# A new start for a Strassen ReGLU kernel: x rows and three weight columns plain on one queue, three plain blocks, second x half in quarter steps

## Chip, cores, metric

One core of one Trainium2 chip. The metric is the device time of one execution in microseconds (us), median of several runs. The engines are named as the profile names them: PE (TensorE), DVE (VectorE), ACT (ScalarE), POOL (GpSimd), SP (the queue of the sync engine). PEld is weight loading.

## The reference

```python
# x: 16 x 256 x 512, w1: 512 x 4096, w2: 2048 x 512, all float32
h = x @ w1
gate, value = np.split(h, 2, axis=-1)
h = np.maximum(gate, 0) * value
return (h @ w2).astype(np.float32)
```

## The kernel before

The 4096 rows of x are done in four sets of 1024. Everything is cast to f16. Both products are done by a Strassen form with seven products instead of eight: sums of weight quarters (T1 to T4) and of x quarters (S1 to S4) are formed first, and a "Block" for one column of 128 gates and 128 values then takes 14 matmuls of 512 columns. A "Plain" block needs no sums and takes 16. The first set begins with plain blocks, because the sums take time. What a block yields, max(gate, 0) times value, is called g; the second product needs sums of g in the same way, here "g sums". In the lines of the profile, wr are the plain weights and wt their sums, x_A the plain quarters of x and x_S their sums, g_S the sums of g (at the start these buffers, and g, also hold loaded float32 data); W, X and Y are the accumulators that PE writes.

```python
WX = {"P1": ("B11", "A11"), "P2": ("B21", "A12"), "P3": ("B22", "S4"), "P4": ("T4", "A22"),
      "P5": ("T1", "S1"), "P6": ("T2", "S2"), "P7": ("T3", "S3")}       # weight, x
SLOT = {"P1": 0, "P5": 1, "P2": 3, "P6": 4, "P3": 5, "P7": 9, "P4": 13}  # a block every 7 slots
SUMS = (("S1", "A21", "A22", SUB), ("S2", "S1", "A11", SUB), ("S4", "A12", "S2", ADD), ("S3", "A11", "A21", SUB))
# ... cut ...
NFILL = 2
NPLAIN = 4
CHUNKS = ((0, 2), (2, 2), (4, 2), (6, 2), (8, 4), (12, 4))     # weight columns by chunk
```

The x sums of the first set are made by VectorE, each a sum of two SBUF tensors of 128 x 1024 f16. The start of the first set, shortened:

```python
for i in range(2):                                   # SP queue, float32
    nc.sync.dma_start(out=xf[:, 2 * i:2 * i + 2], in_=x_v[0, :, 2 * i:2 * i + 2])
    nc.sync.dma_start(out=wl[:, :, i], in_=w1_v[:, :, i, :2 * P])
nc.gpsimd.tensor_copy(out=gate, in_=xf[:, 0, :1])    # GpSimd's casting loads wait for the first x
fetch_w1(1, 0); fetch_w1(1, 1)                       # casting loads on GpSimd's queue
# ... second half of x, casting, then the other chunks of w1 ...
# ... casts, transposes, plain blocks of the first x half ...
for p in plain:                                      # second x half, four plain blocks
    # ... matmuls ...
    x_sum(xo)                                        # VectorE: one of S1, S2, S4, S3
    if p is not plain[-1]:
        p.close(1)
    look_x(0, p.jb)
```

GpSimd makes the weight sums of the first set, and issues the loads of w2 between them:

```python
w1_ops(nc.gpsimd, 4, 2)       # T1..T4 for columns 4 and 5: four instructions of 128 x 512
fetch_w2(0)
fetch_w2(1)
w1_ops(nc.gpsimd, 6, 2)
fetch_w2(2)
fetch_w2(3)
w1_ops(nc.gpsimd, 8, 2)
w1_ops(nc.gpsimd, 10, 2)
# ... copies of w2 ...
for t in TURNS:
    w1_one(nc.gpsimd, 12, 4, *t)
    if t[0] == "T2":
        add_w2("T1", "B12"); add_w2("T3", "B22")
add_w2("T2", "T1")
cast_x(1)
# ... later, at P2 of columns 11, 13, 15 (h = 0, 2, 4): sums for the second matmul
for m in ("S1", "S3")[:2 - h // 4]:
    g_sum(nc.gpsimd, go, m, h, h + 2)
# ... and at the end of the set:
g_sum(nc.vector, go, "S1", 6, 8)
for m in ("S2", "S4"):
    for h in (0, NHC // 2):
        g_sum(nc.vector, go, m, h, h + NHC // 2)
g_sum(nc.vector, go, "S3", NHC // 2, NHC)
```

Of the kernel before, what the change touches and what calls it, by code (L numbers as in the profile page):

```python
# [20 lines left out]
NFILL = 2  # L21
NPLAIN = 4
# [77 lines left out]
def fast_way(ctx, tc, x2, w1, w2, out2, flag):  # L100
# [26 lines left out]
    CHUNKS = ((0, 2), (2, 2), (4, 2), (6, 2), (8, 4), (12, 4))  # L127
# [27 lines left out]
    def w1_ops(eng, jb, n):  # L155
        for t in TURNS:
            w1_one(eng, jb, n, *t)
# [37 lines left out]
    class Block:  # L195
        def __init__(self, xo, g, jb):
            self.xo, self.g, self.jb = xo, g, jb
# [46 lines left out]
    class Plain:  # L244
        def __init__(self, g, jb):
            self.g, self.jb = g, jb

        def open_x(self):
            self.X = psx.tile([P, TH], F32, name="X", tag="X")

        def open_w(self):
            self.W = psw.tile([P, TH], F32, name="W", tag="W")

        def mm(self, side, a, q, n=1):
            ts = slice(q * 256, (q + n) * 256)
            ps = self.W if side else self.X
            for e in range(4):
                name = (("B11", "B21"), ("B12", "B22"))[side][e // 2]
                nc.tensor.matmul(ps[:, ts], W(name, self.jb)[:, e % 2], a[:, e, ts], start=e == 0, stop=e == 3,  # L259
                                 skip_group_check=True)  # L260

        def close(self, h):
            v = tmp.tile([P, 2, TH], F32, name="v", tag="tmp")[:, 0]
            nc.scalar.activation(v, self.W, COPY, scale=GS)
            nc.vector.scalar_tensor_tensor(out=self.g[:, self.jb, h * TH:(h + 1) * TH], in0=self.X, scalar=0.0,
                                           in1=v, op0=MAX, op1=MULT)
# [12 lines left out]
    def mm2_stream(s, go):  # L279
# [14 lines left out]
        def step(name, b):  # L294
# [19 lines left out]
            elif name == "P3":  # L314
# [3 lines left out]
                nc.sync.dma_start(out=out_v[s, 0, b], in_=d["o1"])  # L318
# [48 lines left out]
    xf = go["S1"].rearrange("p a t -> p (a t)").bitcast(F32).rearrange("p (b d) -> p b d", b=NB)  # L367
    xh = go["S2"][:, :NB]
    wl = g[:, NJ - 4:].rearrange("p a t -> p (a t)").bitcast(F32).rearrange("p (e g j) -> p e g j", e=4, g=2)

    def turn_pair(o, b0):
        for b in (b0, b0 + 1):
            ps = psw.tile([P, 4, P], F32, name="W", tag="W")
            for e in range(4):
                nc.tensor.transpose(ps[:, e], xf[:, b, e * P:(e + 1) * P], ident[F32])
            copy = nc.scalar.copy if b % 2 else nc.vector.tensor_copy
            copy(out=o["A1"][:, :, b * P:(b + 1) * P], in_=ps)  # L377

    def turn_half(o, b0, copy):
        ps = psx.tile([P, 4, 2, P], F16, name="X", tag="X")  # L380
# [9 lines left out]
    def cast_w(g_):  # L390
        nc.scalar.copy(out=wr[0][:, :2, g_], in_=wl[:, :2, g_])
        nc.vector.tensor_copy(out=wr[0][:, 2:, g_], in_=wl[:, 2:, g_])  # L392
# [12 lines left out]
    for i in range(2):  # L405
        nc.sync.dma_start(out=xf[:, 2 * i:2 * i + 2], in_=x_v[0, :, 2 * i:2 * i + 2])  # L406
        nc.sync.dma_start(out=wl[:, :, i], in_=w1_v[:, :, i, :2 * P])
    for t in ident.values():
        make_identity(nc, t)
    nc.gpsimd.tensor_copy(out=gate, in_=xf[:, 0, :1])  # L410
    fetch_w1(1, 0)
    fetch_w1(1, 1)
    for b in (0, 2):
        nc.gpsimd.dma_start(out=xh[:, b:b + 2], in_=x_v[0, :, NB + b:NB + b + 2])
# [5 lines left out]
    plain = [Plain(g, jb) for jb in range(NPLAIN)]  # L420
    idle(NWARM)
    cast_w(0)
    turn_pair(xo, 0)
    idle(NFILL)
    plain[0].open_x()
    plain[1].open_x()
    for p in plain[:2]:
        p.mm(0, xo["A1"], 0)
    cast_w(1)
    turn_pair(xo, 2)  # L430
    for p in plain[:2]:
        p.open_w()
        p.mm(1, xo["A1"], 0)
    for p in plain[:2]:
        p.mm(0, xo["A1"], 1)
        p.mm(1, xo["A1"], 1)
        p.close(0)
    for p in plain[2:]:
        p.open_x()
        p.open_w()  # L440
        p.mm(0, xo["A1"], 0, 2)
        p.mm(1, xo["A1"], 0, 2)
        p.close(0)
        if p is plain[2]:
            turn_half(xo, 0, nc.vector.tensor_copy)
    turn_half(xo, 2, nc.scalar.copy)
# [6 lines left out]
    for p in plain:  # L453
        p.open_x()
        p.open_w()
        if p is plain[0]:
            for q in range(2):
                p.mm(0, xo["A2"], q)
                p.mm(1, xo["A2"], q)
        else:  # L460
            p.mm(0, xo["A2"], 0, 2)
            p.mm(1, xo["A2"], 0, 2)
        x_sum(xo)
        if p is not plain[-1]:
            p.close(1)
        look_x(0, p.jb)

    def look_w1(i):
        c, o = place[i // 2 * 2]
        look(wr[c][:, :, i % 2, o * P:(o + 2) * P], NX + i, 1024)  # L470
# [27 lines left out]
    LOOKS[0, NPLAIN].insert(0, lambda: plain[-1].close(1))  # L498
# [15 lines left out]
    for s in range(NS):  # L514
# [4 lines left out]
        plan = {jb * PERIOD + at: (jb, n) for jb in blocks for n, at in SLOT.items()}  # L519
        last = NJ * PERIOD  # L520
        stream = mm2_stream(s, go)
        if s == 0:
            w1_ops(nc.gpsimd, 4, 2)
            fetch_w2(0)
            fetch_w2(1)
            w1_ops(nc.gpsimd, 6, 2)
# [53 lines left out]
        if s + 1 < NS:  # L580
# [9 lines left out]
            if s == 0:  # L590
                w1_ops(nc.vector, 0, 2)
                w1_ops(nc.vector, 2, 2)
# [33 lines left out]
```

## Time and profile before

| | before |
|---|---|
| median of three runs | 312.16 us (311.8 to 312.37) |
| span of the profiled run | 310.2 us |
| PE busy | 301.7 us |
| granted PE clock | 1.0 |

From the profile's page of the kernel before, the busy time of each engine and the chain that ended last by engine:

```profile
PE 301.7 (97%) x1867; PEld 183.0 (59%) x1867; DVE 216.4 (70%) x330; ACT 189.0 (61%) x450; POOL 148.3 (48%) x135
...
PE 92%; DMA 2%; DVE 2%; issue 1%; ACT 1%; SPq 0%; DVEq 0%
```

PE is busy 97% of the span, and the chain that ended last is 92% PE. What can be won lies in PE's few waits. The timeline of PE shows them; its columns are start in us, length in us, engine, line, operation, output and inputs, count, and in brackets the idle time before it with what ended it. Kernel before, PE's timeline:

```profile
10.68 1.03 PE L259 MATMUL W<-x_A,wr 128*128 128x256 f16 x8 [1.51 <-DVE x_A L377]
...
18.95 0.60 PE L259 MATMUL X<-x_A,wr 128*128 128x256 f16 x4 [0.27 <-ACT x_A L384]
...
25.43 0.59 PE L202 MATMUL W<-x_S,wt 128*128 128x512 f16 x2
26.25 0.59 PE L202 MATMUL X<-x_A,wr 128*128 128x512 f16 x2 [0.23 <-ACT Y L209]
...
27.54 0.59 PE L202 MATMUL X<-x_A,wr 128*128 128x512 f16 x2
```

The stalls are 1.51, 0.27 and 0.23 us. Matmuls of 512 start every 0.216 us, so a product of two takes 0.432. P5 of column 4 (25.43) is its second product, P2 (26.25) its third, and P1 of column 5 starts at 27.54.

Kernel before, VectorE's timeline, its four x sums S1, S2, S4, S3 (written x_S):

```profile
18.93 1.54 DVE L451 TENSOR_TENSOR x_S<-x_A 128x1024 f16<-128x1024 f16 x1 [0.21 <-ACT x_A L384]
...
21.25 0.78 DVE L451 TENSOR_TENSOR x_S<-x_S,x_A 128x1024 f16<-128x1024 f16 x1
...
22.98 0.68 DVE L451 TENSOR_TENSOR x_S<-x_A,x_S 128x1024 f16<-128x1024 f16 x1
...
24.71 0.68 DVE L451 TENSOR_TENSOR x_S<-x_A,x_A 128x1024 f16<-128x1024 f16 x1
```

GpSimd's timeline over the same stretch, weight sums (wt) and the issue of two w2 loads:

```profile
19.88 1.60 POOL L160 TENSOR_TENSOR wt<-wr 128x512 f16<-128x512 f16 x1
21.44 1.60 POOL L160 TENSOR_TENSOR wt<-wr,wt 128x512 f16<-128x512 f16 x1
22.99 1.81 POOL L356 DMA_DIRECT2D w<-in_w_dram  x2
24.80 1.59 POOL L160 TENSOR_TENSOR wt<-wr 128x512 f16<-128x512 f16 x1
26.47 1.15 POOL L160 TENSOR_TENSOR wt<-wr,wt 128x512 f16<-128x512 f16 x1
```

S1 took 1.54 us. GpSimd's sums of the same shape took 1.15 to 1.16 us when undisturbed, and 1.60, 1.60 and 1.59 where a VectorE sum had begun before them.

### The profile page before, as it was taken

To read this page: it belongs to the slowest core of one execution; us is meant where nothing else is said; L and a number is where in the kernel's file an instruction comes from. 1 tells how busy PE (TensorE), PEld (TensorE's weight loads), DVE (VectorE), ACT (ScalarE), POOL (GpSimd) and SP (SyncE) were. 2 spreads that over 40 slices of the span, in tenths; PEclk is the share of its full clock that TensorE was granted. 3 is DMA by queue.
4 is the path that set the end of the run, shared out by engine and by line. 5 is a ranking of instruction groups with operands and counts; after the bars stand their busy time and mean duration, and the time that the engine had idled before them with its cause. 6 is when DMAs were issued, how large, how long until landed. Compare 5 with 4: busy or idle time off the path is not lost.

```text
span 310.2 us, 5097 instructions
## 1 busy us (share of the span) xinstructions
PE 301.7 (97%) x1867; PEld 183.0 (59%) x1867; DVE 216.4 (70%) x330; ACT 189.0 (61%) x450; POOL 148.3 (48%) x135
## 2 busy tenths in 40 slices
PE   8899999999999999999999999999999999999993
PEld 4654444588854444478874444458884444448883
DVE  1376888898548888884338888886526888888311
ACT  3347767647677667648847667656857667673230
POOL 5779997950003537992001435995000433898000
PEclk9999999999999999999999999999999999999999
DMA  7999979998315370045220110028311100000113
GB/s 246 200 202 204 215 195 231 203 120 231 121 73 101 71 169 0 3 92 158 90 104 35 34 34 2 0 52 151 139 71 68 34 6 30 0 2 0 69 68 139
DMA packets 33449, 30.74 MB, mean 99 GB/s; under 512 B 13872, under 2 KB 27952, under 8 KB 33200
## 3 DMA queue, kind: packets, MB, share of 16 engines
q0 software_dynamic: 10704, 11.54, 23.1%
q1 hardware_dynamic: 22576, 18.75, 20.5%
q8 instruction: 15, 0.25, 0.4%
q10 hardware_dynamic: 144, 0.13, 0.1%
q14 instruction: 10, 0.08, 0.1%
HBM read 24.12 MB, written 11.53 MB: 115 GB/s over the span
## 4 chain that ended last, share of the span: by engine, by line
PE 92%; DMA 2%; DVE 2%; issue 1%; ACT 1%; SPq 0%; DVEq 0%
PE Y L202 25%; PE X L202 17%; PE W L202 17%; PE Y L286 13%; PE W L286 8%; PE X L286 8%; DMA g<-in_w_dram 2%; PE W L259 2%; PE X L259 2%; DVE g_S L275 1%; ACT x_A L384 0%; SPq L406 0%; DVE wr L392 0%; DVE g L241 0%; DVE x_A L377 0%
## 5 line engine op out<-in xcount | busy, mean ns | idle before, releaser
L275 POOL TENSOR_TENSOR g_S<-g 128x512 f16<-128x512 f16 (+1 forms) x47 | 60.5, 1330 | 125.3 <-DVE g L241 123.4
L202 PEld LDWEIGHTS <-wt 128*128 128x128 f16 x480 | 46.9, 98 | 55.0 <-issue 0.2
L202 PE MATMUL X<-x_A,wr 128*128 128x512 f16 x240 | 71.4, 379 | 0.2 <-ACT Y L209 0.2
L202 PE MATMUL Y<-x_S,wt 128*128 128x512 f16 x240 | 71.4, 379 | 0.0
L202 PEld LDWEIGHTS <-wr 128*128 128x128 f16 x360 | 35.2, 98 | 41.1 <-issue 0.5
L229 DVE SCALAR_TENSOR_TENSOR cc<-W,pu 128x512 f32<-128x512 f32 x60 | 41.5, 692 | 23.8 <-ACT pu L223 23.7
L209 ACT COPY Y<-X 128x512 f32<-128x512 f32 x60 | 34.2, 570 | 37.7 <-PE X L202 37.1
L286 PEld LDWEIGHTS <-g_S 128*128 128x128 f16 x512 | 49.9, 98 | 6.4 <-DVE g_S L275 0.6
L235 DVE SCALAR_TENSOR_TENSOR cc<-Y,pu 128x512 f32<-128x512 f32 x60 | 41.5, 691 | 6.2 <-PE Y L202 0.2
L223 ACT ACTIVATE pu<-Y 128x512 f32<-128x512 f32 x60 | 35.8, 597 | 14.3 <-PE Y L202 14.3
L230 DVE SCALAR_TENSOR_TENSOR g<-X,cc 128x512 f16<-128x512 f32 x60 | 41.5, 691 | 2.3
L286 PEld LDWEIGHTS <-g 128*128 128x128 f16 x384 | 37.6, 98 | 8.2
L241 DVE SCALAR_TENSOR_TENSOR g<-Y,cc 128x512 f16<-128x512 f32 x60 | 40.8, 681 | 1.8 <-PE Y L202 1.8
L216 ACT ACTIVATE pu<-W 128x512 f32<-128x512 f32 x60 | 36.1, 602 | 0.0
L202 PE MATMUL W<-x_S,wr 128*128 128x512 f16 x120 | 35.7, 379 | 0.0
L202 PE MATMUL W<-x_S,wt 128*128 128x512 f16 x120 | 35.7, 379 | 0.0
L202 PE MATMUL Y<-x_A,wt 128*128 128x512 f16 x120 | 35.7, 379 | 0.0
L286 PE MATMUL X<-w,g 128*128 128x256 f16 x256 | 31.2, 272 | 0.0
L286 PE MATMUL Y<-v,g_S 128*128 128x256 f16 x256 | 30.6, 273 | 0.0
L316 DVE SCALAR_TENSOR_TENSOR o<-W,pv 128x256 f32<-128x256 f32 x16 | 6.8, 423 | 30.4 <-PE W L286 30.4
L275 POOL TENSOR_TENSOR g_S<-g,g_S 128x512 f16<-128x512 f16 x18 | 21.8, 1210 | 1.4
L275 POOL TENSOR_TENSOR g_S<-g_S,g 128x512 f16<-128x512 f16 x18 | 21.3, 1186 | 1.4
(69 smaller groups left out, 297.4 us busy)
## 6 DMA issues: line engine op xcount, KB each, us to landing
out_dram<-o SPq DMA_DIRECT2D x16, 256.0 KB, 2.2
out_dram<-pv SPq DMA_DIRECT2D x15, 256.0 KB, 2.0
x<-in_x_dram POOLq DMA_DIRECT2D x3, 1024.0 KB, 8.0
xn<-x SPq DMA_DIRECT2D x12, 256.0 KB, 3.2
wr<-in_w_dram POOLq DMA_DIRECT2D x4, 512.0 KB, 14.5
w<-in_w_dram POOLq DMA_DIRECT2D x4, 512.0 KB, 11.8
wr<-in_w_dram POOLq DMA_DIRECT2D x6, 256.0 KB, 8.8
g_S<-in_x_dram SPq DMA_DIRECT2D x2, 512.0 KB, 4.7
```

The lines of the kernel that those rows point to most:

```text
L202: nc.tensor.matmul(ps, W(wn, self.jb)[:, b], self.xo[xn][:, b, :], start=fresh and b == 0, stop=b == 1, skip_group_check=True)
L209: nc.scalar.copy(out=self.Y, in_=self.X)
L216: nc.scalar.activation(self.p5, self.W, COPY, scale=GS)
L223: nc.scalar.activation(self.u2, self.Y, COPY, scale=-GS)
L229: nc.vector.scalar_tensor_tensor(out=self.c12, in0=self.W, scalar=GS, in1=self.u2, op0=MULT, op1=ADD)
L230: nc.vector.scalar_tensor_tensor(out=self.g[:, self.jb, :TH], in0=self.X, scalar=0.0, in1=self.c12, op0=MAX, op1=MULT)
L235: nc.vector.scalar_tensor_tensor(out=self.c22, in0=self.Y, scalar=-GS, in1=self.p5, op0=MULT, op1=ADD)
L241: nc.vector.scalar_tensor_tensor(out=self.g[:, self.jb, TH:], in0=self.Y, scalar=0.0, in1=self.c22, op0=MAX, op1=MULT)
L259: nc.tensor.matmul(ps[:, ts], W(name, self.jb)[:, e % 2], a[:, e, ts], start=e == 0, stop=e == 3, skip_group_check=True)
L275: eng.tensor_tensor(go[n][:, h0:h1], go[i0][:, h0:h1], go[i1][:, h0:h1], op=op)
L286: nc.tensor.matmul(ps, go[gn][:, k, b * P:(b + 1) * P], V[vn][:, k, :], start=fresh and k == 0, stop=k == NHC - 1, skip_group_check=True)
L316: nc.vector.scalar_tensor_tensor(out=d["o1"][:, HALF:], in0=d["W"], scalar=1 / GS, in1=d["pu"][:, 1], op0=MULT, op1=ADD)
```

## The change

The intent: have the matmuls start without waiting for a load in the wrong order, and use one plain block fewer. All x rows of the first set and three weight columns come as float32 on the SP queue in order of use, and are cast on chip; three blocks are plain instead of four; the second half of x is used in quarter steps as it arrives; P1 of the first Strassen block (column 3) is done before the last plain values. The core of the diff, cut:

```diff
-NFILL = 2
-NPLAIN = 4
+NFILL = 1
+NPLAIN = 3
-    CHUNKS = ((0, 2), (2, 2), (4, 2), (6, 2), (8, 4), (12, 4))
+    CHUNKS = ((0, 2), (2, 1), (3, 2), (5, 3), (8, 4), (12, 4))
+    for b in (0, 2):
+        nc.sync.dma_start(out=xf[:, b:b + 2], in_=x_v[0, :, b:b + 2])
+    fetch_wl(0, 0)
+    fetch_wl(1, 0)
+    fetch_wl(0, 1, 2)
+    nc.sync.dma_start(out=xg[:, :2], in_=x_v[0, :, NB:NB + 2])
+    fetch_wl(2, 0)
+    fetch_wl(2, 1)
+    nc.sync.dma_start(out=xg[:, 2:], in_=x_v[0, :, NB + 2:])
-    nc.gpsimd.tensor_copy(out=gate, in_=xf[:, 0, :1])
+    nc.gpsimd.tensor_copy(out=gate, in_=wl[0][:, 0, 1, :1])
 # ... cut: the start ...
+    whole[0].values()
+    whole[0].close()
+    cast_w(2, 0)
+    whole[1].values()
+    nc.vector.tensor_copy(out=xh[:, :2], in_=xg[:, :2])
+    turn_half(xo, 0, nc.vector.tensor_copy)
+    whole[1].close()
+    cast_w(2, 1)
+    nc.scalar.copy(out=xh[:, 2:], in_=xg[:, 2:])
+    part(whole[2])
+    part(parts[0][0])
+    part(parts[0][1])
+    turn_half(xo, 2, nc.scalar.copy)
+    part(parts[0][2])
+    x_sum(xo)
+    for p in parts[1][:2]:
+        part(p)
+        x_sum(xo)
+        look_x(0, p.jb)
+    parts[1][2].gates()
+    lead.P1()
+    parts[1][2].values()
+    look_x(0, 2)
+    x_sum(xo)
 # ... cut: GpSimd's order ...
-            w1_ops(nc.gpsimd, 4, 2)
+            w1_ops(nc.gpsimd, 3, 2)
             fetch_w2(0)
             fetch_w2(1)
-            w1_ops(nc.gpsimd, 6, 2)
+            w1_ops(nc.gpsimd, 5, 3)
 # ... cut: the stores of the last set are split in two ...
```

More of the change, by code (lines that the diff above doesn't have):

```diff
@@ L244, in fast_way, with __init__, mm, gates @@
     class Plain:
-        def __init__(self, g, jb):
-            self.g, self.jb = g, jb
-        def open_x(self):
-            self.X = psx.tile([P, TH], F32, name="X", tag="X")
-        def open_w(self):
-            self.W = psw.tile([P, TH], F32, name="W", tag="W")
-        def mm(self, side, a, q, n=1):
-            ts = slice(q * 256, (q + n) * 256)
-            ps = self.W if side else self.X
-            for e in range(4):
-                name = (("B11", "B21"), ("B12", "B22"))[side][e // 2]
-                nc.tensor.matmul(ps[:, ts], W(name, self.jb)[:, e % 2], a[:, e, ts], start=e == 0, stop=e == 3,
-                                 skip_group_check=True)
-        def close(self, h):
-            v = tmp.tile([P, 2, TH], F32, name="v", tag="tmp")[:, 0]
-            nc.scalar.activation(v, self.W, COPY, scale=GS)
-            nc.vector.scalar_tensor_tensor(out=self.g[:, self.jb, h * TH:(h + 1) * TH], in0=self.X, scalar=0.0,
-                                           in1=v, op0=MAX, op1=MULT)
+        def __init__(self, g, jb, a, h, q, n):
+            self.g, self.jb, self.a, self.at, self.q = g, jb, a, h * TH, range(q, q + n)
+            self.t = slice(q * HALF, (q + n) * HALF)
+        def mm(self, ps, names, q):
+            ts = slice(q[0] * HALF, q[-1] * HALF + HALF)
+            for e in range(4):
+                nc.tensor.matmul(ps[:, ts], W(names[e // 2], self.jb)[:, e % 2], self.a[:, e, ts], start=e == 0,
+                                 stop=e == 3, skip_group_check=True)
+        def gates(self, q=None):
+            if q is None or q[0] == self.q[0]:
+                self.X = psx.tile([P, TH], F32, name="X", tag="X")
+            self.mm(self.X, ("B11", "B21"), q or self.q)
+        def values(self):
+            self.W = psw.tile([P, TH], F32, name="W", tag="W")
+            self.mm(self.W, ("B12", "B22"), self.q)
+        def close(self):
+            v = tmp.tile([P, 2, TH], F32, name="v", tag="tmp")[:, 0, self.t]
+            nc.scalar.activation(v, self.W[:, self.t], COPY, scale=GS)
+            nc.vector.scalar_tensor_tensor(out=self.g[:, self.jb, self.at + self.t.start:self.at + self.t.stop],
+                                           in0=self.X[:, self.t], scalar=0.0, in1=v, op0=MAX, op1=MULT)
     def g_ops(g, gs):
@@ L317, in step @@
                                                op0=MULT, op1=ADD)
-                nc.sync.dma_start(out=out_v[s, 0, b], in_=d["o1"])
+                for n in (slice(0, HALF), slice(HALF, DO)) if last and b else (slice(0, DO),):
+                    nc.sync.dma_start(out=out_v[s, 0, b, :, n], in_=d["o1"][:, n])
             elif name == "P7":
@@ L366, in fast_way, with turn_pair @@
     g, go = g_tiles()
-    xf = go["S1"].rearrange("p a t -> p (a t)").bitcast(F32).rearrange("p (b d) -> p b d", b=NB)
-    xh = go["S2"][:, :NB]
-    wl = g[:, NJ - 4:].rearrange("p a t -> p (a t)").bitcast(F32).rearrange("p (e g j) -> p e g j", e=4, g=2)
-    def turn_pair(o, b0):
+    xf, xg = (go[n].rearrange("p a t -> p (a t)").bitcast(F32).rearrange("p (b d) -> p b d", b=NB) for n in ("S1", "S2"))
+    xh = go["S4"][:, :NB]
+    wl = [g[:, j0:j1].rearrange("p a t -> p (a t)").bitcast(F32).rearrange("p (e g j) -> p e g j", e=4, g=2)
+          for j0, j1 in ((NJ - 4, NJ), (NJ - 6, NJ - 4))]
+    def turn_pair(o, b0, pool, nm):
         for b in (b0, b0 + 1):
-            ps = psw.tile([P, 4, P], F32, name="W", tag="W")
+            ps = pool.tile([P, 4, P], F32, name=nm, tag=nm)
             for e in range(4):
@@ L379, in turn_half @@
     def turn_half(o, b0, copy):
-        ps = psx.tile([P, 4, 2, P], F16, name="X", tag="X")
+        ps = psw.tile([P, 4, 2, P], F16, name="W", tag="W")
         for b in range(2):
@@ L388, in turn_by_dma, with cast_w, fetch_wl @@
             nc.sync.dma_start_transpose(out=o[f"A{h + 1}{k + 1}"], in_=x16[s][h * TH:(h + 1) * TH, k * 256:k * 256 + 256])
-    def cast_w(g_):
-        nc.scalar.copy(out=wr[0][:, :2, g_], in_=wl[:, :2, g_])
-        nc.vector.tensor_copy(out=wr[0][:, 2:, g_], in_=wl[:, 2:, g_])
+    def cast_w(jb, g_):
+        c, i = place[jb]
+        for es, copy in ((slice(0, 2), nc.scalar.copy), (slice(2, 4), nc.vector.tensor_copy)):
+            copy(out=wr[c][:, es, g_, i * P:(i + 1) * P], in_=wl[c][:, es, g_, i * P:(i + 1) * P])
+    def fetch_wl(jb, g_, n=1):
+        c, i = place[jb]
+        nc.sync.dma_start(out=wl[c][:, :, g_, i * P:(i + n) * P], in_=w1_v[:, :, g_, jb * P:(jb + n) * P])
     rows = {}
@@ L403, in look_x @@
         look(t[:, i % 2 * 256:i % 2 * 256 + 256], 4 * NB * s + i, 256)
-    for i in range(2):
-        nc.sync.dma_start(out=xf[:, 2 * i:2 * i + 2], in_=x_v[0, :, 2 * i:2 * i + 2])
-        nc.sync.dma_start(out=wl[:, :, i], in_=w1_v[:, :, i, :2 * P])
+    for b in (0, 2):
[7 more added lines that the diff above has]
+    nc.sync.dma_start(out=xg[:, 2:], in_=x_v[0, :, NB + 2:])
     for t in ident.values():
         make_identity(nc, t)
-    nc.gpsimd.tensor_copy(out=gate, in_=xf[:, 0, :1])
-    fetch_w1(1, 0)
-    fetch_w1(1, 1)
-    for b in (0, 2):
-        nc.gpsimd.dma_start(out=xh[:, b:b + 2], in_=x_v[0, :, NB + b:NB + b + 2])
+    nc.gpsimd.tensor_copy(out=gate, in_=wl[0][:, 0, 1, :1])
     for c in range(2, len(CHUNKS)):
@@ L419, in fast_way @@
     xo = x_tiles()
-    plain = [Plain(g, jb) for jb in range(NPLAIN)]
-    idle(NWARM)
-    cast_w(0)
-    turn_pair(xo, 0)
-    idle(NFILL)
-    plain[0].open_x()
-    plain[1].open_x()
-    for p in plain[:2]:
-        p.mm(0, xo["A1"], 0)
-    cast_w(1)
-    turn_pair(xo, 2)
-    for p in plain[:2]:
-        p.open_w()
-        p.mm(1, xo["A1"], 0)
-    for p in plain[:2]:
-        p.mm(0, xo["A1"], 1)
-        p.mm(1, xo["A1"], 1)
-        p.close(0)
-    for p in plain[2:]:
-        p.open_x()
-        p.open_w()
-        p.mm(0, xo["A1"], 0, 2)
-        p.mm(1, xo["A1"], 0, 2)
-        p.close(0)
-        if p is plain[2]:
-            turn_half(xo, 0, nc.vector.tensor_copy)
-    turn_half(xo, 2, nc.scalar.copy)
+    whole = [Plain(g, jb, xo["A1"], 0, 0, 2) for jb in range(NPLAIN)]
+    parts = [[Plain(g, jb, xo["A2"], 1, q, 1) for jb in range(NPLAIN)] for q in range(2)]
+    lead = Block(xo, g, NPLAIN)
     sums = list(SUMS)
@@ L451, in x_sum, with part, look_w1 @@
         nc.vector.tensor_tensor(o[n], o[i0], o[i1], op=op)
-    for p in plain:
-        p.open_x()
-        p.open_w()
-        if p is plain[0]:
-            for q in range(2):
-                p.mm(0, xo["A2"], q)
-                p.mm(1, xo["A2"], q)
-        else:
-            p.mm(0, xo["A2"], 0, 2)
-            p.mm(1, xo["A2"], 0, 2)
-        x_sum(xo)
-        if p is not plain[-1]:
-            p.close(1)
-        look_x(0, p.jb)
-    def look_w1(i):
-        c, o = place[i // 2 * 2]
-        look(wr[c][:, :, i % 2, o * P:(o + 2) * P], NX + i, 1024)
+    def part(p):
+        p.gates()
+        p.values()
+        p.close()
+    idle(NWARM)
+    turn_pair(xo, 0, psw, "W")
+    cast_w(0, 0)
+    idle(NFILL)
+    turn_pair(xo, 2, psx, "X")
+    whole[0].gates((0,))
+    cast_w(1, 0)
+    whole[0].gates((1,))
+    whole[1].gates()
+    cast_w(0, 1)
+    cast_w(1, 1)
+    whole[0].values()
[22 more added lines that the diff above has]
+    x_sum(xo)
+    def look_w1(i):
+        if CHUNKS[place[i // 2 * 2][0]][1] % 2 == 0 and i // 2 != 2 or i // 2 == 3:
+            c, o = place[i // 2 * 2]
+            t = wr[c][:, :, i % 2, o * P:(o + 2) * P]
+        else:
+            c, o = place[i // 2 * 2 + i % 2]
+            t = wr[c].rearrange("p e g j -> p (e g) j")[:, :, o * P:(o + 1) * P]
+        look(t, NX + i, 1024)
     def look_w2(i):
@@ L497, in fast_way @@
                 LOOKS[s, i] = [lambda s=s, i=i: look_x(s, i)]
-    LOOKS[0, NPLAIN].insert(0, lambda: plain[-1].close(1))
+    LOOKS[0, NPLAIN].insert(0, parts[1][2].close)
     for s in range(NS - 1):
@@ L518, in fast_way @@
         blocks = {jb: Block(xo, g, jb) for jb in range(first, NJ)}
-        plan = {jb * PERIOD + at: (jb, n) for jb in blocks for n, at in SLOT.items()}
+        if s == 0:
+            blocks[first] = lead
+        plan = {jb * PERIOD + at: (jb, n) for jb in blocks for n, at in SLOT.items() if (s, jb, n) != (0, first, "P1")}
         last = NJ * PERIOD
@@ L591, in fast_way @@
                 w1_ops(nc.vector, 0, 2)
-                w1_ops(nc.vector, 2, 2)
+                w1_ops(nc.vector, 2, 1)
             advance(stream, MM2 - TAIL - 100 - done)
```

## The prediction

> **What bounds the kernel.** TensorE. The page's busy line has PE at 301.7 of 310.2 us, and the chain that ended last is 92% PE. Outside the start (4.7 us before the first transposes) and the tail (4.7 us after the last matmul), the timeline shows only about 2 us of PE stalls, all early: 1.51 us at 10.68 (value weights land at 9.2, then a cast and a transposed copy that queue behind one another), 0.27 at 18.95, 0.23 at 26.25. So only the first 27 us and the tail can move; granted clock is 1.0 throughout.
>
> **What the change removes.** One plain column: 16 matmuls of 512 (3.46 us at the 0.216 us pitch) become a Strassen block of 14 (3.02 us): -0.43. The 1.5 us stall should go, because the x rows and column weights now come in order of use. The software queue has 1 MB less to cast (it moved about 200 KB/us; the hardware queue 350 KB/us alone).
>
> **What it adds.** Casts on ScalarE and VectorE, each in program order:
> - second-half x: a 128x1024 f32 cast, about 0.75 us (estimate from the 0.43 us 128x512 cast; up to 1.3 if contended, as the 0.81 us one was), before its transposes;
> - column weights, about 0.35 us per half-column piece.
>
> **Arrivals** (estimates from bytes moved per us in the DMA records plus 0.5 us to landing): first x pair 4.3, second 5.7, gate weights 6.6 and 7.5, values 9.1, third x pair 10.5, third column 11.4 and 12.3, last x pair 14.0. DMA is then not the limit; the VectorE order is.
>
> **New stalls on PE, worked out:**
> 1. Gates of the second quarter wait for ScalarE's copy of the fourth transposed block: 0.35 us.
> 2. After the second column's values, PE goes to the f16 transposes of x. Their cast sits on VectorE behind the first product (which waits for ScalarE: 0.2+0.6, then 0.61) and the third column's cast: PE idles 1.7 to 2.4 us, near 11.5.
> 3. Third column's values: their VectorE cast is behind the transposed copy (0.6) and the second product (0.61): about 1.0 us, near 15.
> 4. Second x half's ScalarE copy (1.0 us) against 0.86 us of cover: 0.4 us.
> 5. The early P1 needs an X bank that VectorE frees only after the first x sum (1.54 us before, beside GpSimd): 0 to 0.7 us.
>
> Sum about 4.1 us (3.4 to 5.5). PE work alone, from the first transposes at 4.67: 1.71+0.2+0.87+10.37+0.88+0.43 = 14.5, so P5 of the first Strassen block would start at 19.1 without stalls, 23.2 with. Before's steady pattern, set back one block, is matched at 22.8. Net about +0.4 us. GpSimd's first T sums should be ready by 17 to 21, in time. A stall near 2 us should not cool the array: the Trainium skill ("TensorE: Matmul & The Clock Gate", Part 1) puts that at an idle window of about 3.4 us, and before's 1.5 us stall left matmuls at full rate.
>
> **Tail.** The last PE work, copy and store are unchanged; splitting other final stores in two adds issues off the chain: 0.
>
> **Prediction: 312.4 us, 311.3 to 313.6 (8 in 10). Faster by over 2%: 0.01; within 2%: 0.98; slower: 0.01.**
>
> **Right if** the timeline shows PE idle near 11.5 ended by the copied x cast (VectorE), near 15 by the third column's cast, P5 of the first Strassen block (column 3) near 23, and the old 1.5 us stall gone; PE busy about 0.6 us lower. **Wrong if** VectorE's casts run at the slow rate or the 512-byte weight rows land late (slower), if GpSimd's sums come after 23 (slower), if the array cools, or if casts and copies overlap better than I read, leaving under 2.5 us of stalls (faster by 1 us).

## The result and the profile after

| | before | after |
|---|---|---|
| median | 312.19 us (311.8 to 312.37, 4 runs) | 317.17 us (316.32 to 317.9, 4 runs) |
| span of the profiled run | 310.2 us | 314.4 us |
| PE busy | 301.7 us | 301.0 us |

The ratio is 1.016 (95% interval 1.0133 to 1.0188). Ratios here are the mean time of one kernel's fast runs over the mean of the other's in the same rounds, so they are not quite the ratio of the quoted medians. The profiled run of the changed kernel was its fastest (316.32 us), so the profile shows 4.2 of the 5.0 us.

From the page after:

```profile
PE 301.0 (96%) x1868; PEld 181.9 (58%) x1868; DVE 222.5 (71%) x340; ACT 191.8 (61%) x459; POOL 146.7 (47%) x131
...
PE 90%; DVE 4%; DMA 2%; issue 1%; SPq 1%; ACT 1%; ACTq 0%
```

PE has less to do, as intended, and the chain now has 4% of VectorE in it. The stretch that differs is found at once with the busy time by engine from 22 to 32 us. Kernel before, then after:

```profile
core 0: us, PE busy (x) PEld busy (x) DVE busy (x) ACT busy (x) POOL busy (x), PEclk, DMA share, GB/s
22.00:32.00 10.00, 9.77 (x46) 4.37 (x45) 6.66 (x11) 7.53 (x21) 9.90 (x10) 1.00 1.29 204
```

```profile
core 0: us, PE busy (x) PEld busy (x) DVE busy (x) ACT busy (x) POOL busy (x), PEclk, DMA share, GB/s
22.00:32.00 10.00, 6.31 (x29) 2.63 (x29) 9.95 (x10) 5.13 (x15) 9.92 (x8) 1.00 1.29 204
```

PE loses 3.5 us of work in these 10 us, VectorE goes from 6.66 to 9.95 busy, and GpSimd is busy throughout in both. The timeline of PE after answers to the one of before:

```profile
7.15 1.97 PE L252 MATMUL X<-x_A,wr 128*128 128x256 f16 x12 [0.30 <-ACT wr L397]
9.90 1.90 PE L252 MATMUL W<-x_A,wr 128*128 128x512 f16 x8 [0.79 <-ACT wr L397]
13.48 0.62 PE L387 MATMUL W<-ident,g_S 128*128 128x128 f16 x8 [1.68 <-DVE g_S L460]
...
15.69 0.60 PE L252 MATMUL W<-x_A,wr 128*128 128x512 f16 x2 [0.29 <-DVE wr L397]
...
22.95 0.59 PE L202 MATMUL W<-x_S,wt 128*128 128x512 f16 x2
23.38 0.59 PE L202 MATMUL X<-x_A,wr 128*128 128x512 f16 x2
25.17 0.59 PE L202 MATMUL Y<-x_S,wt 128*128 128x512 f16 x2 [1.20 <-DVE x_S L438]
27.31 0.59 PE L202 MATMUL W<-x_S,wr 128*128 128x512 f16 x2 [1.54 <-DVE x_S L438]
...
28.17 0.59 PE L202 MATMUL W<-x_S,wt 128*128 128x512 f16 x2
29.35 0.59 PE L202 MATMUL Y<-x_S,wt 128*128 128x512 f16 x2 [0.59 <-DVE x_S L438]
...
31.51 0.59 PE L202 MATMUL Y<-x_A,wt 128*128 128x512 f16 x2 [0.28 <-DVE cc L235]
31.94 0.59 PE L202 MATMUL X<-x_A,wr 128*128 128x512 f16 x2
```

The row at 22.95 is P5 of column 3, the first Strassen block, and the row at 31.94 is P1 of column 5. Between them lie eleven products, 4.75 us of work; it took 8.99. From the starts, the stalls are 1.36 us before P6, 1.71 before P3, 0.75 before P7 and 0.44 before P4 of column 3: 4.26 us. (The brackets show less, as they count from the modelled end of the matmul before.) Three of the four waits end with an x sum on VectorE. P1 of column 5 is 4.4 us later than before, and the last copy ends 3.8 us later, so the rest of the kernel added nothing.

VectorE after, the same four x sums:

```profile
20.19 1.50 DVE L438 TENSOR_TENSOR x_S<-x_A 128x1024 f16<-128x1024 f16 x1
...
21.95 3.17 DVE L438 TENSOR_TENSOR x_S<-x_S,x_A 128x1024 f16<-128x1024 f16 x1
...
25.38 1.78 DVE L438 TENSOR_TENSOR x_S<-x_A,x_S 128x1024 f16<-128x1024 f16 x1
27.09 2.12 DVE L438 TENSOR_TENSOR x_S<-x_A,x_A 128x1024 f16<-128x1024 f16 x1
```

GpSimd after, over the same stretch:

```profile
21.08 1.81 POOL L359 DMA_DIRECT2D w<-in_w_dram  x2
22.89 1.67 POOL L160 TENSOR_TENSOR wt<-wr 128x768 f16<-128x768 f16 x1
24.64 1.97 POOL L160 TENSOR_TENSOR wt<-wr,wt 128x768 f16<-128x768 f16 x1
26.58 2.08 POOL L160 TENSOR_TENSOR wt<-wr 128x768 f16<-128x768 f16 x1
```

S2, S4 and S3 took 3.17, 1.78 and 2.12 us, against 0.78, 0.68 and 0.68 before. The weight sums for columns 5 to 7 are 128 x 768 now and run beside them. S2 begins at 21.95, when GpSimd is still issuing two loads (21.08 to 22.89), and ends at 25.12, 0.56 us after the first weight sum: so of the 2.5 us that it lost, 0.9 passed beside the issue of loads and the rest beside the weight sum. S4 begins at 25.38 while GpSimd is at a weight sum that ends at 26.61; S4 ends at 27.16, less than an undisturbed sum's 0.68 us later. GpSimd's next sum, begun at 26.58, takes 2.08 us, where the same sum undisturbed takes 1.64 (in e1). The two take turns.

### The profile page after: what moved, and what is told of

Its sections match the earlier page's. It is cut to its first block, busy times and chain, and to the rows that moved or that the text cites. A ratio compares the mean times of both kernels' runs of the same rounds, so it can differ in the third digit from the quotient of the medians.

```text
span 314.4 us, 5121 instructions
## 1 busy us (share of the span) xinstructions
PE 301.0 (96%) x1868; PEld 181.9 (58%) x1868; DVE 222.5 (71%) x340; ACT 191.8 (61%) x459; POOL 146.7 (47%) x131
## 4 chain that ended last, share of the span: by engine, by line
PE 90%; DVE 4%; DMA 2%; issue 1%; SPq 1%; ACT 1%; ACTq 0%
PE Y L202 25%; PE X L202 16%; PE W L202 16%; PE Y L288 13%; PE W L288 9%; PE X L288 9%; DVE x_S L438 2%; DMA g<-in_w_dram 2%; PE W L252 1%; DVE g L267 1%; PE W L387 0%; ACT v L266 0%; SPq L401 0%; DVE g_S L460 0%; SPq L415 0%
## 5 line engine op out<-in xcount | busy, mean ns | idle before, releaser
L277 POOL TENSOR_TENSOR g_S<-g 128x512 f16<-128x512 f16 (+1 forms) x47 | 59.4, 1272 | 130.4 <-DVE g L241 126.8
L202 PEld LDWEIGHTS <-wt 128*128 128x128 f16 x488 | 47.7, 98 | 58.3 <-issue 2.0
L202 PE MATMUL Y<-x_S,wt 128*128 128x512 f16 x244 | 72.6, 379 | 1.8 <-DVE x_S L438 1.8
L202 PE MATMUL X<-x_A,wr 128*128 128x512 f16 x244 | 72.5, 379 | 0.2 <-DVE g L267 0.2
L229 DVE SCALAR_TENSOR_TENSOR cc<-W,pu 128x512 f32<-128x512 f32 x61 | 42.2, 691 | 23.2 <-ACT pu L223 23.0
L235 DVE SCALAR_TENSOR_TENSOR cc<-Y,pu 128x512 f32<-128x512 f32 x61 | 42.2, 691 | 6.9 <-PE Y L202 0.5
L230 DVE SCALAR_TENSOR_TENSOR g<-X,cc 128x512 f16<-128x512 f32 x61 | 42.2, 691 | 2.3
L241 DVE SCALAR_TENSOR_TENSOR g<-Y,cc 128x512 f16<-128x512 f32 x61 | 41.6, 682 | 1.8 <-PE Y L202 1.8
L216 ACT ACTIVATE pu<-W 128x512 f32<-128x512 f32 x61 | 36.8, 603 | 0.0
```

The lines of the kernel that those rows point to most:

```text
L202: nc.tensor.matmul(ps, W(wn, self.jb)[:, b], self.xo[xn][:, b, :], start=fresh and b == 0, stop=b == 1, skip_group_check=True)
L216: nc.scalar.activation(self.p5, self.W, COPY, scale=GS)
L229: nc.vector.scalar_tensor_tensor(out=self.c12, in0=self.W, scalar=GS, in1=self.u2, op0=MULT, op1=ADD)
L230: nc.vector.scalar_tensor_tensor(out=self.g[:, self.jb, :TH], in0=self.X, scalar=0.0, in1=self.c12, op0=MAX, op1=MULT)
L235: nc.vector.scalar_tensor_tensor(out=self.c22, in0=self.Y, scalar=-GS, in1=self.p5, op0=MULT, op1=ADD)
L241: nc.vector.scalar_tensor_tensor(out=self.g[:, self.jb, TH:], in0=self.Y, scalar=0.0, in1=self.c22, op0=MAX, op1=MULT)
```

## The experiments

Theory A: the x sums on VectorE are blocked by GpSimd's weight sums, for the length of an instruction, through the SBUF port that they share. The Trainium skill, page "SBUF — State Buffer", section "Who interferes with whom", says that a VectorE instruction with two SBUF inputs contends with a GpSimd instruction that reads SBUF, and that the shared ports are an exclusive lock: whoever issues first has them for the whole instruction and the other blocks fully (this it says of VectorE's 2-port modes; that it holds for these sums is what e1 to e3 test). Rivals: the sums are stretched by the loads (B); the sums are merely too late, because the change packs the plain blocks tighter (C); the one long queue is late with its loads (D, E).

The table gives for each kernel what its own profile shows: the start of the first cast of gate weights on ScalarE (when they had landed, or when ScalarE was free), the start of P5 of the first Strassen column, the stall from there to P1 of column 5 (the time between less 4.75 us), that P1, and PE's waits after 40 us. Kernels with the start of before have four plain columns, so only their column 5 can be compared.

| kernel | gate cast | P5 | stall | P1 of col. 5 | waits after 40 us | median | ratio |
|---|---|---|---|---|---|---|---|
| before | 6.02 | 25.43 | | 27.54 | 0.34 | 312.19 | |
| after | 6.69 | 22.95 | 4.24 | 31.94 | 0 | 317.17 | 1.016 |
| e1 GpSimd held | 8.22 | 24.08 | 0.17 | 29.00 | 0.87 | 314.63 | 1.0096 |
| e2 four loads in a row | 6.93 | 22.79 | 0.57 | 28.11 | 0 | 313.44 | 1.006 |
| e3 narrow weight sums | 8.96 | 24.56 | 0.27 | 29.58 | 0.58 | 313.72 | 1.0049 |
| e5 e2, paired gate load | 9.06 | 23.89 | 0.57 | 29.21 | 0.35 | 313.64 | 1.0076 |
| e8 half sums earlier | 6.75 | 26.76 | 0.18 | 31.69 | 0 | 317.08 | 1.017 |
| e6 VectorE reordered | 6.68 | 21.12 | 0.18 | 26.05 | 1.21 | 312.29 | 1.0019 |
| e12 e6, one g sum moved | 6.94 | 20.42 | 0.18 | 25.35 | 0.85 | 310.83 | 0.997 |

### e1: GpSimd held beside the x sums

```diff
             w1_ops(nc.gpsimd, 3, 2)
+            nc.gpsimd.tensor_copy(out=gate, in_=xo["S3"][:, 0, :1])
             fetch_w2(0)
```

> The changed kernel, with GpSimd held (by a one-element copy that reads the last x sum) between its sums for columns 3-4 and its next work, so that nothing of GpSimd's runs beside x sums S2, S4 and S3. Theory A (the x sums on VectorE lose the SBUF port they share with GpSimd, so they took 3.17, 1.78 and 2.12 us beside its weight sums): they fall to 0.7 us each, TensorE's stalls before P6, P3, P7 and P4 of the first Strassen blocks (4.3 us together) fall under 0.6 us, and the time is 312.5 to 313.7 us, a ratio of about 1.003 to before. Rival B (the sums are stretched by the loads' writes into SBUF, or by ScalarE): the loads go on, so S2 to S3 stay over 1.5 us each and the time stays near 317. Rival C (the sums are late because the tail of the plain blocks is packed tighter, not because they are longer): sums 0.7 us or not, the stalls stay above 2 us.

Measured: 314.63 us (314.42 to 315.79), ratio 1.0096. VectorE's timeline of this run:

```profile
23.08 0.68 DVE L438 TENSOR_TENSOR x_S<-x_S,x_A 128x1024 f16<-128x1024 f16 x1
...
24.01 0.68 DVE L438 TENSOR_TENSOR x_S<-x_A,x_S 128x1024 f16<-128x1024 f16 x1
24.61 0.68 DVE L438 TENSOR_TENSOR x_S<-x_A,x_A 128x1024 f16<-128x1024 f16 x1
```

S2, S4 and S3 took 0.68 us each, and the stall fell from 4.24 to 0.17 us, with the casting loads running as before (201 to 216 GB/s in each us from 22 to 25, against 202 to 210 in the changed kernel). That bears out theory A, except that the hold keeps back GpSimd's issue of loads as well as its weight sums (e2 parts the two); rivals B and C fall. Something of C stays, though: even at 0.68 us each sum is done only 0.7 to 1.4 us before its product starts here; in the kernel before it was 3.0 to 4.7 us. The time is 1 us above the expected range. Two things made that up in the profiled run: the first gate weights came 1.5 us later than in the changed kernel's profile, and 0.87 us of new waits appeared at 71 us (see e6).

### e2: four loads in a row, then the weight sums

```diff
             w1_ops(nc.gpsimd, 3, 2)
-            fetch_w2(0)
-            fetch_w2(1)
+            for i in range(4):
+                fetch_w2(i)
             w1_ops(nc.gpsimd, 5, 3)
-            fetch_w2(2)
-            fetch_w2(3)
```

> The changed kernel, with all four w2 loads issued by GpSimd in a row (3.6 us of descriptor work) before its sums for columns 5-7, so that descriptor work and no weight sum runs beside S2 to S3. Theory A as far as GpSimd's reading instructions go (descriptor work does not hold the port against a two-input sum): S2, S4, S3 at 0.7 to 0.8 us, time 312.5 to 313.7 us, as with the hold. Theory A2 (descriptor work blocks VectorE's sums too, since S2 started at 21.95 while GpSimd issued loads and yet was not done when the next weight sum began at 22.89): S2 takes 2.5 to 3.5 us, and the time falls by 2 us at most, to 315 or more. Rival B: no change, near 317.

Measured: 313.44 us (312.44 to 314.78), ratio 1.006: of the 5 us, 3.7 by the medians or about 3.1 by the ratios are back, by a reordering of GpSimd's instructions alone. VectorE's timeline,

```profile
21.80 1.78 DVE L438 TENSOR_TENSOR x_S<-x_S,x_A 128x1024 f16<-128x1024 f16 x1
...
23.84 0.68 DVE L438 TENSOR_TENSOR x_S<-x_A,x_S 128x1024 f16<-128x1024 f16 x1
24.44 0.68 DVE L438 TENSOR_TENSOR x_S<-x_A,x_A 128x1024 f16<-128x1024 f16 x1
```

and GpSimd's:

```profile
20.93 3.56 POOL L359 DMA_DIRECT2D w<-in_w_dram  x4
24.47 2.14 POOL L160 TENSOR_TENSOR wt<-wr 128x768 f16<-128x768 f16 x1
```

S4 and S3 are at 0.68 us. S2 took 1.78 us while GpSimd did nothing but issue loads, so the expectation that descriptor work leaves a two-input sum alone was missed for that one. In e5, with the same order, it was 1.79 again; in e3 S2 ran at 0.68 in the same place between two loads. So a sum beside the issue of loads can take about 1.1 us longer, as S2 of the changed kernel did at its beginning, but when it does was not settled.

### e3: narrow weight sums

```diff
-            w1_ops(nc.gpsimd, 5, 3)
+            for jb in (5, 6, 7):
+                w1_ops(nc.gpsimd, jb, 1)
```

> The changed kernel, with the weight sums of columns 5-7 done one column at a time on GpSimd (12 instructions of about 0.65 us, an estimate from 1.15 us for 512 elements and 1.65 for 768, in place of 4 of 1.7 to 2.1 us). If the port is held for a whole instruction, a VectorE sum waits for one short instruction: S2 under 2.2 us, S4 and S3 under 1.4 us, time down by 1.5 to 3 us, to 314 to 315.7. If the engines instead share a rate, the sums stay as long as they were (3.2, 1.8, 2.1) and so does the time, near 317.

Measured: 313.72 us (313.18 to 314.66), ratio 1.0049, a little better than expected. S2, S4 and S3 took 0.68, 1.27 and 1.16 us. GpSimd's timeline beside them:

```profile
24.51 0.70 POOL L160 TENSOR_TENSOR wt<-wr 128x256 f16<-128x256 f16 x1
25.28 1.01 POOL L160 TENSOR_TENSOR wt<-wr,wt 128x256 f16<-128x256 f16 x1
26.26 1.11 POOL L160 TENSOR_TENSOR wt<-wr 128x256 f16<-128x256 f16 x1
```

A narrow sum takes 0.66 to 0.70 us where nothing was in its way, and 1.01 and 1.11 where VectorE went first. With short instructions on the other side, the wait is short: the port is held by the instruction, and its length is the price. The total work of GpSimd grew a little and the time still fell by 3.5 us.

### e4: the kernel before, made to collide

```diff
             w1_ops(nc.gpsimd, 4, 2)
-            fetch_w2(0)
-            fetch_w2(1)
             w1_ops(nc.gpsimd, 6, 2)
+            fetch_w2(0)
+            fetch_w2(1)
```

> The kernel BEFORE, with its two w2 loads moved from between GpSimd's weight sums of columns 4-5 and 6-7 to after both, so that its x sums S4 and S3 (0.68 us each, at 22.98 and 24.71) fall beside weight sums as in the changed kernel. Theory A: the three sums after S1 grow to over 1.2 us on average. The time grows by only 0 to 1.5 us, since TensorE needs S2 at 26.7 and S3 at 28.4, some 3 us after they were done: the kernel before had both a free port and slack. If the sums do not grow, theory A is wrong for this place.

Measured: 313.93 us (313.7 to 314.12), ratio 1.0059. The x sums took 0.89, 0.73 and 0.68 us: the expected growth did not come. GpSimd's four weight sums in this stretch took 1.60, 1.60, 1.61 and 1.60 us instead of 1.15. Here VectorE's sums come at a distance of about 1.7 us and GpSimd's every 1.6; each x sum was ready when a weight sum ended, went first, and GpSimd paid. So in the start of before the contention was there too, but it fell on the engine that had time. It need not fall there: in the profile of e13 below, with the same start, S2, S4 and S3 took 1.47, 1.04 and 1.04 us, and PE did not wait for them, since they were still done 2.5 to 4.0 us before their products. The long sums cost the changed kernel time because it had lost this slack too. The 2 us lost in e4 come later, as its profile shows: GpSimd's sums for columns 12 to 15 were late (PE waits of 0.55 and 0.17 us at 53 and 55 us), and the g sums on VectorE (0.52 and 0.35 at 71 and 73). GpSimd itself had waited 3.76 us for a copy of w2 just before, against 2.36 in the kernel before: this edit also issues the first w2 loads 5.7 us later. It is the chain of these loads and GpSimd's work together that has little slack.

### e5: the first gate weights as one paired load

On top of e2:

```diff
-    fetch_wl(0, 0)
-    fetch_wl(1, 0)
+    fetch_wl(0, 0, 2)
     fetch_wl(0, 1, 2)
```

> The kernel with four loads in a row (e2), and the gate weights of columns 0 and 1 loaded as one 512 KB transfer with 1 KB rows in place of two of 256 KB with 512-byte rows. In the four profiles so far of kernels with the single-column loads the first gate cast started at 6.7, 8.2, 6.9 and 9.0 us, the values cast at 9.4, 10.6, 9.3 and 11.3 us; in the two profiles with paired loads at 6.0, 6.6 and 9.2, 9.3. Theory D (the 512-byte rows are what comes late and unevenly): first gate cast 7.0 to 7.6, values cast 9.1 to 9.5, and the timed runs spread less than 1 us; time 312.3 to 313.3. Rival E (one of the 16 engines lags in some executions whatever the row, and a queue with 3.5 MB on it shows it longer): casts still up to 2 us late in some execution, spread of the timed runs over 1.5 us, time as e2, about 313.4.

Measured: 313.64 us (312.6 to 317.27), ratio 1.0076 (interval 1.0002 to 1.015). The gate cast started at 9.06 us, as late as the worst with short rows, and the spread was 4.7 us. Theory D falls: the short rows are not what comes late. In the first 7 us the loads of the changed kernel, e1 and e3 moved 235, 232 and 227 GB/s, nearly the same, though their gates were cast at 6.69, 8.22 and 8.96. The bytes arrive at nearly the same pace and the load still completes late. (In e5 itself it was 213 GB/s.) The Trainium skill, "DMA: Bandwidth & Descriptors", section "Why a DMA increments its semaphore by 16 and not by 1", says that a load is complete only when all of up to 16 engines are through with their share. One lagging engine would look like this (rival E); the trace does not name the engines, so it stays argued. Kernels with the start of before were steadier: 312.06 us median, 311.67 to 312.64 in eleven runs.

### e8: half of each x sum earlier

```diff
     part(whole[2])
+    x_half(0, ("S1", "S2", "S3", "S4"))      # columns 0..255; the other halves where the sums were
```

> The changed kernel, GpSimd's order untouched, with the first half of each x sum (columns 0 to 255 of the half set) done while VectorE idles near 16 us, so that half of the sums' work leaves the contested stretch. Theory A with slack: a half sum near 16 us takes 0.36 us free or waits for the rest of one GpSimd instruction; the late halves are as often blocked as before but shorter by 0.35 us each: TensorE's stalls fall from 4.3 to 2.5-3.5 us, time 315.5 to 316.5. If the length of the sums themselves were the matter and not the blocking, the stalls would halve or better: under 2.2 us, time under 315.

Measured: 317.08 us (315.92 to 317.81), ratio 1.017: no gain. My placing was wrong. VectorE works in program order, and the half sums stood behind the third column's product; they began at 17.35 us, not near 16, when GpSimd had begun its weight sums. They took 0.42, 1.26, 1.25 and 1.37 us. The stall moved ahead of P5: PE waited 2.89 us at 22.03 for VectorE's products, P5 started at 26.76, and after it the stall was 0.18. The wait was not all: after it PE ran at a granted clock of 0.50 to 0.54 until about 25.4 us, with a group of four matmuls of 256 every 0.85 us in place of 0.44. Between the group at 18.54 and P5, e8 lost 4.0 us more than the changed kernel, an estimate from the starts: 2.7 by more waiting and 1.6 by the slow clock, less 0.3 for a wait of the changed kernel that is gone. That the half sums were stretched beside weight sums fits theory A; that the total comes out level with the changed kernel is chance.

### e7: the split stores alone

```diff
-                nc.sync.dma_start(out=out_v[s, 0, b], in_=d["o1"])
+                for n in (slice(0, HALF), slice(HALF, DO)) if last and b else (slice(0, DO),):
+                    nc.sync.dma_start(out=out_v[s, 0, b, :, n], in_=d["o1"][:, n])
```

> The kernel BEFORE with only the split of the last stores from the change. The prediction gave it 0: within 0.3 us of before, ratio 0.999 to 1.001. A rival that puts part of the loss in the tail: 0.5 us or more slower.

Measured: the kernel before with this one part of the change took 312.34 us (312.19 to 313.01), ratio 1.0009 (interval 0.9993 to 1.0026). The tail is worth nothing either way, as predicted.

### e6: VectorE in the order of need

On top of e2: the cast of x before the first product, both casts of the third column before the transposed copy, half sums placed before GpSimd's sums begin, column 5's weight sums apart.

```diff
+    nc.vector.tensor_copy(out=xh[:, :2], in_=xg[:, :2])
     whole[0].values()
     whole[0].close()
     cast_w(2, 0)
     whole[1].values()
-    nc.vector.tensor_copy(out=xh[:, :2], in_=xg[:, :2])
-    turn_half(xo, 0, nc.vector.tensor_copy)
-    whole[1].close()
-    cast_w(2, 1)
+    v = whole[1].scale()                     # ScalarE's half of close()
+    cast_w(2, 1)
+    turn_half(xo, 0, nc.vector.tensor_copy)
+    whole[1].product(v)                      # VectorE's half
+    x_half(0, ("S1", "S2", "S3", "S4"))
 # ...
-            w1_ops(nc.gpsimd, 5, 3)
+            w1_ops(nc.gpsimd, 5, 1)
+            w1_ops(nc.gpsimd, 6, 2)
```

> e2 with VectorE's start put in the order of need: the cast of x ahead of the first product, both casts of the third column ahead of the transposed copy, x sums in two halves, the first half before GpSimd's sums begin; weight sums of column 5 apart. If the prediction's terms 2 and 3 (1.68 us near 11.5 and 0.29 us near 15 in the trace) are real waits on VectorE's order, the first goes, TensorE starts P5 of column 3 about 2 us earlier than in e2 (22.8 by its trace) and the time is 310.5 to 312, at or below before. If the loads set the pace instead, the stall moves to the third column's weights and the time stays at 312.8 to 313.6.

Measured: 312.29 us (312.12 to 313.38), ratio 1.0019: level with before, a little above the range. The predicted waits of 1.68 and 0.29 us are gone, so they were what the prediction said; P1 of column 5 starts at 26.05, 1.5 us ahead of before. PE's timeline shows where that went:

```profile
51.41 0.61 PE L202 MATMUL Y<-x_S,wt 128*128 128x512 f16 x2 [0.16 <-POOL wt L160]
...
69.06 1.48 PE L294 MATMUL Y<-v,g_S 128*128 128x256 f16 x12 [0.53 <-DVE g_S L283]
...
71.33 1.48 PE L294 MATMUL W<-w,g_S 128*128 128x256 f16 x12 [0.35 <-DVE g_S L283]
```

PE waits for GpSimd's weight sums of columns 12 to 15, and for VectorE's g sums, of which the first (63.95 us, 2.79 us long) stood beside GpSimd's last one (63.15 to 66.18). A better start runs into a later floor.

### e9, e10, e11: an attempt to shorten GpSimd's later chain

On top of e6 (e9), on the kernel before (e10), and e9 with GpSimd's loads let go earlier (e11):

```diff
-            for t in TURNS:
-                w1_one(nc.gpsimd, 12, 4, *t)
-                if t[0] == "T2":
-                    add_w2("T1", "B12")
-                    add_w2("T3", "B22")
-            add_w2("T2", "T1")
+            w1_ops(nc.gpsimd, 12, 4)
+            add_w2("T1", "B12")
+            add_w2("T3", "B22")
             cast_x(1)
 # ... add_w2("T2", "T1") now at column 13; g sum S3 rows 2-3 moved to VectorE
 # e11 only:
-    nc.gpsimd.tensor_copy(out=gate, in_=wl[0][:, 0, 1, :1])
+    nc.gpsimd.tensor_copy(out=gate, in_=wl[0][:, 0, 0, P:P + 1])
```

> e6 with GpSimd's later chain shortened: its sums for columns 12-15 are no longer split by the w2 additions, and one g sum (rows 2-3 of S3) goes to VectorE. In e6 TensorE was 1.5 us ahead of before at column 5 (26.05 against 27.54 us) and lost 1.2 us again, at 51-53 us to GpSimd's weight sums (0.33 us) and at 69-71 us to the g sums (0.88 us, before had 0.34). Theory F (GpSimd's chain, which starts with the loads and does not follow TensorE's gain, is the next floor and eats what the start wins): both stalls fall under 0.3 us together and the time is 310.3 to 311.5 us, 0.3 to 0.5% under before. Rival G (the late loss of e6 has another source): the stalls move or stay, time 312 or more.

> The kernel BEFORE with the same shortening of GpSimd's later chain and nothing of the start. Before lost only 0.34 us there in its profile (0.88 in the profile of the kernel with split stores, whose start is the same): time 311.3 to 312.0, ratio 0.998 to 1.0. If it gains more than 0.8 us, the gain of e9 would be no merit of the start.

> e9 with GpSimd's load issue let go by the second load of gate weights (landing near 7.5 us) in place of the values' (near 9.5). Its casting loads and with them its sums should come 1.5 to 2 us earlier, at the price of sharing the engines with the last x rows, which land 0.3 to 0.8 us later. Theory F: as e9 or up to 0.5 us faster, 310.0 to 311.3. If instead the last x rows become late for the second transposes, a stall over 0.4 us appears near 16 us and it is no faster than e9.

Measured: 318.42 us (ratio 1.0224), 314.44 us (1.0099) and 318.08 us (1.0212). All three missed, by an error of mine: the addition T2 now stood behind the 1 MB cast of x on the same queue, the addition T4 waited for it, and GpSimd stood still for 7.5 to 8.6 us. In e9 PE waited for it:

```profile
71.23 2.74 PE L294 MATMUL W<-v_T,g_S 128*128 128x256 f16 x12 [5.40 <-POOL g_S L283]
```

The weight sum waits at 51 and 53 us did disappear, but the runs say nothing about the g sum. One by-product: these 12 matmuls of 256 took 2.74 us where the same group takes 1.48 elsewhere. After 5.4 us of idleness the array was at half rate (granted clock 0.50). The Trainium skill, "TensorE: Matmul & The Clock Gate", Part 1, puts the limit at a window of about 3.4 us. Here less was enough: the wait of 2.89 us in e8, 3.05 from the starts, left the array at half rate, while waits of 1.68 us (changed kernel), 1.91 (e10) and 2.61 (e3, at 9.42 us) left the matmuls after them at full pace.

### e12 and e13: one g sum moved, and its control

Only this, on e6 (e12) and on the kernel before (e13):

```diff
-                    for m in ("S1", "S3")[:2 - h // 4]:
+                    for m in ("S1", "S3")[:2 - (h > 0)]:
                         g_sum(nc.gpsimd, go, m, h, h + 2)
 # ...
-            g_sum(nc.vector, go, "S3", NHC // 2, NHC)
+            g_sum(nc.vector, go, "S3", 2, NHC)
```

> e6 with one edit later on: rows 2-3 of the g sum S3 go from GpSimd to VectorE, so that GpSimd's last g sum ends near 63.5 us in place of 66.2 and VectorE's first one, at 64, need not wait for it (2.79 us in e6). e9 and e11 tried this with the w2 additions moved as well, and failed for a reason of my making: an addition that waits for another was queued behind the 1 MB x cast on the same queue, held GpSimd 8 us and TensorE 5.4. Theory F (GpSimd's later chain eats what the start wins): the stalls at 69-71 us (0.88 us) go, the time is 311.0 to 311.8 us, at or up to 0.3% under before. Rival G: the stalls stay or move, 312.2 or more.

> The kernel BEFORE with the same one edit. It has 0.34 us to win in its first profile: 311.3 to 311.9, ratio 0.997 to 1.0. If it wins as much as e12 loses less, the start of the change is worth nothing even when repaired: then e12 and e13 come within 0.4 us of each other.

Measured: e12 310.83 us (310.5 to 312.6, 6 runs), ratio 0.997 (0.9948 to 0.9991); e13 311.14 us (310.77 to 311.7, 6 runs), ratio 0.9972 (0.9958 to 0.9985). Both beat both kernels. The first g sum on VectorE now takes 0.72 and 0.69 us, and the waits near 70 us are gone in both. In e12 waits of 0.68 and 0.17 us at 51 and 53 us remain; the first of them:

```profile
51.23 0.61 PE L202 MATMUL Y<-x_S,wt 128*128 128x512 f16 x2 [0.68 <-ACT pu L216]
```

(It is laid to ScalarE by the profile, but a weight sum of GpSimd's ended at 51.18, just before it.) At column 5 e12 is 1.77 us ahead of e13 (25.35 against 27.12); at the last copy 0.62 (303.96 against 304.58); in the medians 0.3, with ranges that overlap. GpSimd's later chain takes most of what the repaired start wins, as theory F said: by the starts of the matmuls, the two waits at 51 and 53 us come to 1.18 us, and the lead shrank by 1.15. The chain is not GpSimd's work alone: at 48 us it waits 1.84 us for a copy of w2 in e12, and 2.15 in e13. A gain of the start in the timed runs is not shown.

## Why the prediction was wrong, point by point

**What bounds the kernel.** Right: PE, with all of the stalls before 27 us but one of 0.34 at 71.

**Stalls up to P5.** Right in sum. P5 of the first Strassen column was predicted at 23.2 us and came at 22.95. Term by term, predicted and measured: first gates 0.35 and 0.30 (by luck: the cause was the cast of the first weights, not the fourth transposed copy); x cast 1.7 to 2.4 and 1.68; third column's values about 1.0 and 0.29 (only the second half of the cast was late, and two matmuls ran first); second x half 0.4 and 0.23; the early P1 0 to 0.7 and 0.15. One of 0.79 us was not foreseen: the first values, whose weights landed at 9.4 instead of 9.1; it made up for the third column's values, put 0.7 too high, so that the sum fits this well is partly luck. The old stall of 1.51 us was gone, as said.

**The step that failed** is the sum of term list and yardstick: "P5 of the first Strassen block would start at 19.1 without stalls, 23.2 with. Before's steady pattern, set back one block, is matched at 22.8. Net about +0.4 us." This takes for granted that from P5 on the pattern is steady. It was not: 4.26 us of stalls followed in the next nine, because S2, S4 and S3 were not ready. The list prices only the first x sum ("1.54 us before, beside GpSimd") and takes for the others, silently, the 0.68 to 0.78 us of before. Before, those were short because S2 and S3 went first at their turn and S4 met only an issue of loads, and they had 3 us and more to spare; after, S2 came beside GpSimd's issue of loads and then a weight sum, S4 and S3 beside wider weight sums, with little to spare. With GpSimd held (e1) they are 0.68 us and the stall is 0.17. The term that was missing is three x sums beside GpSimd: 3.17 + 1.78 + 2.12 in place of 0.78 + 0.68 + 0.68 us, 4.9 us of VectorE's time, of which PE felt 4.26 (0.44 of it at P4, behind a VectorE product queued after the sums).

**"GpSimd's first T sums should be ready by 17 to 21, in time"**: right (the first ended at 17.69, the fourth at 21.15). The prediction asked whether GpSimd's sums were in time and not what they cost the engine beside them.

**The tail at 0**: right (e7).

**Loads**: landings were foreseen within half a microsecond for the profiled run of the changed kernel. That the same loads complete up to 2.3 us later in other executions (6.7 to 9.0 us) was not foreseen. The repaired kernels e2, e3 and e5 stay 1 to 2 us above before, and this is part of it in the profiles of e3 and e5; in the profile of e2 the loads were on time.

**PE busy 0.6 us lower**: 0.7 (301.7 to 301.0).

## What to carry to other kernels

When an instruction is moved in time, its length has to be read again beside what the other engine will be doing there: a two-input sum on VectorE took 0.68 us alone and up to 3.17 beside GpSimd. If such a pair must overlap, make the instructions of the less urgent engine short, or put its work that does not read there; the reordering in e2 gave back 3 to 3.7 of 5 us. And ask how long before its use the result is ready: the start of before bore sums of 1.04 to 1.47 us without a wait (e13). And before rebuilding a start, look for the next floor: here the chain of w2 loads and GpSimd's work at 48 to 71 us took most of a start that was 1.8 us ahead, while moving one sum off that chain (e13) won 0.9 us without touching the start.

## What the Trainium skill lacked or had wrong

- "SBUF — State Buffer", "Who interferes with whom": it says that a two-input VectorE instruction contends with a GpSimd instruction that reads SBUF, not with one that only writes, and infers that descriptor generation does not disturb a `tensor_tensor`. A sum of 0.68 us took 1.78 and 1.79 us in two runs (e2, e5) beside nothing but the issue of loads by GpSimd; in a third (e3) it took 0.68. The profile's spans on GpSimd are rough, so the cause is open, but the statement is not safe to plan on. The whole-instruction lock itself agrees with e1 and e3.
- The same page says that whoever starts first blocks the other. What it lacks is the steady picture when both have a row of such sums: they take turns, the late one waits for the rest of one instruction, and which engine pays depends on how the two rows meet (before: GpSimd, 1.60 instead of 1.15 us; after: VectorE, 1.78 and 2.12 instead of 0.68; e13, with the start of before: both, VectorE 1.04 to 1.47).
- "GPSIMD Engine Reference", "Engine selection", puts a two-input sum on GpSimd at about twice VectorE's time (the page's measured example is float32). Here 128 x 1024 f16 took 2.13 us on GpSimd and 0.68 on VectorE, 3.1 times.
- "DMA: Bandwidth & Descriptors" gives a fixed cost for a load, but no spread from one execution to the next: the first gate weights of kernels with the same loads were cast at 6.7 to 9.0 us at nearly the same rate of bytes (227 to 242 GB/s in the first 7 us).
